# A two-layer mixer encoder: early gates' weights, residual stores, modulations and last down tiles rearranged

## The chip, the cores and the metric

The kernel runs on one core of one Trainium2 chip. The time is the device time of one execution in microseconds; three runs of the kernel before gave a median of 3291.7 us (3289.4 to 3296.47). Engines are called TensorE (PE in the rows; PEld is its weight load), VectorE (DVE), ScalarE (ACT), GpSimd (POOL) and SyncE (SP, which issues most DMAs).

## The reference

A trunk of two layers on x of 1024 tokens by 1024 features, all in float32. Each layer adds two gated sub-layers to x. Six vectors (shift, scale and gate of each) come from a conditioning vector c.

```python
D_MODEL = 1024; SEQ = 1024; DEPTH = 2; D_FF = 2816
for l in range(DEPTH):
    mod = (c_act @ w_mod[l] + b_mod[l])[:, None, :]
    sh1, sc1, g1, sh2, sc2, g2 = jnp.split(mod, 6, axis=-1)
    h = rms_norm(x, norm_g[l, 0]) * (1 + sc1) + sh1
    parts = jnp.split(h @ w_in[l], split_idx, axis=-1)
    # oa: windowed attention, ob: gated short convolution, oc: latent attention, od: dilated attention
    y = jnp.concatenate([oa, ob, oc, od], axis=-1) @ w_out[l]
    x = x + g1 * rms_norm(y, norm_g[l, 1])
    h = rms_norm(x, norm_g[l, 2]) * (1 + sc2) + sh2
    u = dwconv3(h @ w_up[l], ffn_conv[l])
    ug, uv = jnp.split(u, 2, axis=-1)
    y = (jax.nn.gelu(ug, approximate=True) * uv) @ w_down[l]
    x = x + g2 * rms_norm(y, norm_g[l, 3])
```

## The kernel before

Activations lie transposed: features on the 128 partitions in eight tiles, tokens along the free axis in two halves of 512 (`HALVES`). Each float32 product is three matmuls: both operands are split into a high and a low part (`split`: ScalarE copies the high part, L110, another engine subtracts it, L111; GpSimd where none is named). A layer runs in these stages (us of the profiled execution, layer 0 | layer 1):

- mixer: group A, the rotary tables (layer 0 alone), group D (from 177 | 1837), convolution B, latent attention C (its values from 614 | 2245). `group_d` projects three sets of values and takes a step of the iterator `fill` ahead of each. In layer 0 `fill` is `modulations`: the jobs j = 2, 4, 3 (a gate, a scale, a shift) of layer 0's own modulation. A job is `mod_pieces`, 16 loads of 256 KB (L357) each followed by a multiply-add on VectorE (L360, L362), and `mod_fold`. The loads go into slots of two tiles `room`, which later hold scores of group D.
- `project_out`: the mixer's output projection, first token half, second token half; ScalarE evicts each tile (L1165). Between the halves `residual` (L510 to L515: load of x, scale, add, store to `xd`) and `dense_input` (the norm and the shift, and for the second half the sums that the gates' fast product needs) of the first half run; behind it those of the second half, the *chain* (884 to 944 | 2514 to 2577).
- `dense_up`: 22 gates, each of a gate tile and a value tile of w_up. The product of a gate by two halves of tokens and of features is done with seven quarter products (`quarter`, 12 matmuls each) instead of eight, as in Strassen's scheme. `begin` does two of them, evicted by ScalarE (L1238, L1242). For the first 8 gates (`ahead`) `begin` is run early and its result kept in DRAM (`kept`), so that TensorE has work during the chain; two weights are loaded ahead of the chain (`early`). Then gates 0 and 1 are finished together and gates 2 to 7 one after the other with 60 matmuls, the *kept gates* (about 1012 to 1150 | 2622 to 2760); from gate 8 on `begin` and the rest are run in one, 84 matmuls, the *full gates* (to about 1416 | 3005). `sums` prepares sums of weights on VectorE, `taken` and `tail` read the product banks (L1280, L1281 on ScalarE, L1293 to L1299), `gated` convolves both tiles (`conv3`: L934 on ScalarE or L936 on VectorE, then twice L938), and multiplies the gelu (L1307) of one by the other (L1308, stored at L1309).
- Behind each full gate of layer 0 `advance(3)` issues three of the modulation pieces that `modulate` holds, six jobs: layer 0's j = 5 and layer 1's 1, 0, 2, 4, 3. What is left is issued during the down projection.
- `dense_down`: the 22 tiles of hidden features in chunks. `whole` multiplies a chunk into all eight output tiles; the first chunk is copied to y (L1410), others are added. In layer 0 the last six go by token half, in chunks of two (`some`, adds at L1417), so that layer 0's end and layer 1's start of the first half run beside the second half's products.

The order on each engine is made by a scheduler when the program is built; each engine then runs its own list in order. The DMAs that SP issues wait in SP's list for their slots or data.

Of the kernel before, what the change touches and what calls it, by code (L numbers as in the profile page):

```python
# [92 lines left out]
class Trunk:  # L93
# [369 lines left out]
    def dense_input(self, y, l, half, temp, adders):  # L463
# [20 lines left out]
        for i in range(4):  # L484
# [11 lines left out]
            self.split(self.hh[j][:, n2], self.hl[j][:, n2], b[:, n2])  # L496
# [5 lines left out]
    def residual(self, y, l, g, hs, xsrc, dst, temp, adders=None, rs=None):  # L502
# [3 lines left out]
        for k in range(KT):  # L506
# [8 lines left out]
            nc.sync.dma_start(dst[128 * k:128 * k + 128, hs], yk)  # L515
# [353 lines left out]
    def modulations(self):  # L869

        tiles = [self.sp.tile([128, 2048], F32, name="room", tag=t) for t in ("s10", "s11")]
        room = [t[:, at:at + 512] for t in tiles for at in range(0, 2048, 512)]
        for j in (2, 4, 3):
            pieces = self.mod_pieces(0, j, room)
            try:
                while True:
                    next(pieces)
            except StopIteration as done:
                part = done.value
            yield  # L880
            self.mod_fold(part, room[2])
# [215 lines left out]
    def mixer(self, l):  # L1097
        tc, nc = self.tc, self.nc
        with ExitStack() as e:
# [4 lines left out]
            with ExitStack() as e2:  # L1104
# [9 lines left out]
                self.group_d(l, self.modulations() if l == 0 else iter(()))  # L1114
# [91 lines left out]
    def dense_up(self, l, early):  # L1206
# [12 lines left out]
        ahead = 8  # L1219
        kept = self.kept  # L1220
        with tc.tile_pool(name=f"ux{l}", bufs=2, reuse_waits="tile") as ux, \
# [45 lines left out]
            class Pair:  # L1267
# [21 lines left out]
                def tail(p):  # L1289
# [8 lines left out]
                    nc.gpsimd.tensor_add(uv[:, c2], uv[:, c2], uv[:, c1])  # L1298
# [3 lines left out]
            def gated(t, us):  # L1302
                cv = [self.tmp(x) for x in "ab"]
                for o, u, m in zip(cv, us, (t, FT + t)):
                    base = _P["fconv"] + l * 132 + m
                    self.conv3(o, u, lambda i: self.par[:, base + 44 * i:base + 44 * i + 1], True)
# [33 lines left out]
            for t in range(2, FT):  # L1340
# [8 lines left out]
                if t >= ahead:  # L1349
                    self.advance(3)  # L1350

    def dense_down(self, l, y, end):
# [3 lines left out]
        with tc.tile_pool(name=f"dq{l}", bufs=4, reuse_waits="tile") as dq:  # L1356
# [25 lines left out]
            def load_half(ks, hs, names):  # L1382
# [4 lines left out]
                for k, wd, t in zip(ks, wds, next(room)):  # L1387
# [10 lines left out]
            def whole(ops, first):  # L1398
                for m in range(8):
                    if m:  # L1400
                        self.advance(1 if len(ops) < 4 else 2)
# [7 lines left out]
                    for d, p in [(y[m], po)] if po else [(y[m][:, h], q) for h, q in zip(HALVES, ps)]:  # L1409
                        self.mark = nc.vector.tensor_copy(d, p) if first else nc.vector.tensor_add(d, d, p)  # L1410
# [27 lines left out]
            else:  # L1438
                final, part = [range(at, at + 2) for at in range(k, FT, 2)], slice(0, 512)
                for ks in final:  # L1440
                    some(load_half(ks, HALVES[0], "ppp"), HALVES[0], part)
# [3 lines left out]
                rest = [load_half(ks, HALVES[1], names) for ks, names in zip(final, ("wwq", "qqq", "fff"))]  # L1445
                end(HALVES[0])()
                for ops in rest:
                    some(ops, HALVES[1], part)
                end(HALVES[1])()

    def run(self):
# [47 lines left out]
        for l in range(DEPTH):  # L1499
# [8 lines left out]
            with tc.tile_pool(name=f"fw{l}", bufs=3, reuse_waits="tile") as self.fw:  # L1508
                self.project_out(l, y, token_half(0, t))
                self.turn = cycle((0, 0, 0, 1, 1))  # L1510
                self.pieces = self.modulate([(0, 5), (1, 1), (1, 0), (1, 2), (1, 4), (1, 3)] if l == 0 else [])
                with tc.tile_pool(name=f"te{l}", bufs=1, reuse_waits="tile") as self.te:
                    early = [self.up_weight(l, t) for t in range(2)]
# [94 lines left out]
```

## Time and profile before

| | |
|---|---|
| median of three runs | 3291.7 us |
| lowest, highest | 3289.4, 3296.47 us |
| the profiled execution, its own time | 3296.84 us |
| its span | 3295.0 us |
| its granted TensorE clock, mean | 0.95 of full speed |
| TensorE busy | 2898.2 us (88%) |
| VectorE busy | 2293.4 us (70%) |
| ScalarE busy | 1219.3 us (37%) |
| GpSimd busy | 1208.9 us (37%) |

The profiled execution is one of the kernel as it stands, by the hardware profiler. A row of waits says which instruction stood still, on whose result, and for how long in all, how often, and the longest. A row of a stretch gives its bounds, its length, and each engine's busy time in it.

### The profile page before, as it was taken

To read this page: it belongs to the slowest core of one execution; us is meant where nothing else is said; L and a number is where in the kernel's file an instruction comes from. 1 tells how busy PE (TensorE), PEld (TensorE's weight loads), DVE (VectorE), ACT (ScalarE), POOL (GpSimd) and SP (SyncE) were. 2 spreads that over 40 slices of the span, in tenths; PEclk is the share of its full clock that TensorE was granted. 3 is DMA by queue.
4 is the path that set the end of the run, shared out by engine and by line. 5 is a ranking of instruction groups with operands and counts; after the bars stand their busy time and mean duration, and the time that the engine had idled before them with its cause. 6 is when DMAs were issued, how large, how long until landed. Compare 5 with 4: busy or idle time off the path is not lost. (4 is left out here: it accounts for less than half of the span.)

```text
span 3295.0 us, 35545 instructions
## 1 busy us (share of the span) xinstructions
PE 2898.2 (88%) x13178; PEld 2295.2 (70%) x13178; DVE 2293.4 (70%) x3120; ACT 1219.3 (37%) x1726; POOL 1208.9 (37%) x877
## 2 busy tenths in 40 slices
PE   7888889988858898989888998888897889998997
PEld 3677667776646777768756787677675667776886
DVE  6686666796648777786886735577966696666456
ACT  4222433554433333331233333435534333443121
POOL 1221223224445544552432212242244555555331
PEclk8998999999879999999999999999999899999999
DMA  5235111102423233355431121110123332223323
GB/s 199 80 104 169 55 33 47 39 20 77 147 90 115 94 111 112 107 200 163 160 125 41 52 83 52 42 41 26 52 93 125 115 122 77 77 77 139 129 90 102
DMA packets 124409, 311.62 MB, mean 95 GB/s; under 512 B 13595, under 2 KB 32283, under 8 KB 124236
## 3 DMA queue, kind: packets, MB, share of 16 engines
q1 hardware_dynamic: 121932, 300.97, 27.7%
q10 hardware_dynamic: 2304, 8.39, 0.6%
q8 instruction: 103, 1.69, 0.2%
q14 instruction: 70, 0.57, 0.1%
HBM read 248.58 MB, written 64.13 MB: 95 GB/s over the span
## 5 line engine op out<-in xcount | busy, mean ns | idle before, releaser
L111 POOL TENSOR_TENSOR wl<-raw,wh 128x1024 fp32r<-128x1024 f32 (+2 forms) x82 | 201.4, 2457 | 467.5 <-ACT wh L110 277.1
L530 PE MATMUL pj<-hh,wh 128*128 128x512 f32 x800 | 330.0, 413 | 15.0 <-DVE ql L579 8.4
L531 PE MATMUL pj<-hl,wh 128*128 128x512 f32 x800 | 323.1, 404 | 5.6 <-POOL hl L459 3.9
L534 PE MATMUL pj<-hh,wl 128*128 128x512 f32 x800 | 208.9, 401 | 0.0
L530 PEld LDWEIGHTS pj<-hh,wh 128*128 128x128 f32 x800 | 154.8, 193 | 56.7 <-issue 15.8
L531 PEld LDWEIGHTS pj<-hl,wh 128*128 128x128 f32 x800 | 154.7, 193 | 43.1 <-POOL hl L459 5.5
L534 PEld LDWEIGHTS pj<-hh,wl 128*128 128x128 f32 x800 | 153.0, 192 | 35.6 <-issue 0.9
L690 PE MATMUL po<-s,v 128*96 128x128 f32 (+3 forms) x672 | 130.7, 357 | 45.0 <-ACT s L687 45.0
L111 POOL TENSOR_TENSOR ul<-raw,uh 128x1024 fp32r<-128x1024 f32 x51 | 130.2, 2556 | 93.9 <-ACT uh L110 93.7
L690 PE MATMUL po<-hp,v 128*96 128x256 f32 x512 | 125.0, 399 | 38.3 <-ACT hp L687 38.1
L110 ACT ACTIVATE wh<-raw 128x1024 fp32r<-128x1024 f32 (+2 forms) x90 | 94.1, 1046 | 167.9 <-PE pj L531 76.5
L690 PEld LDWEIGHTS po<-s,v 128*96 128x96 f32 x672 | 98.7, 186 | 71.0 <-ACT s L687 55.7
L577 ACT ACTIVATE qh<-pj 64x512 fp32r<-64x512 f32 x128 | 107.1, 837 | 97.0 <-PE pj L534 51.5
L938 DVE SCALAR_TENSOR_TENSOR ta<-u,par,ta 128x1024 f32<-128x1024 f32 x88 | 135.8, 1543 | 3.4 <-ACT ta L934 3.2
L938 DVE SCALAR_TENSOR_TENSOR tb<-u,par,tb 128x1024 f32<-128x1024 f32 x88 | 136.7, 1553 | 0.3
L579 DVE TENSOR_TENSOR ql<-pj,qh 64x512 fp32r<-64x512 f32 x64 | 55.4, 866 | 116.5 <-ACT qh L577 115.8
L690 PEld LDWEIGHTS po<-hp,v 128*96 128x96 f32 x512 | 85.0, 171 | 72.9 <-ACT hp L687 46.5
L1410 DVE TENSOR_TENSOR y<-y,po 128x1024 f32<-128x1024 f32 x60 | 73.0, 1217 | 87.6 <-PE po L523 87.6
L561 DVE TENSOR_TENSOR ks<-pj,ks 64x512 fp32r<-64x512 f32 x56 | 51.1, 913 | 108.8 <-ACT ks L560 108.2
L111 POOL TENSOR_TENSOR pl<-raw,ph 128x1024 fp32r<-128x1024 f32 x26 | 67.2, 2591 | 147.5 <-ACT ph L110 104.4
L362 DVE SCALAR_TENSOR_TENSOR mc<-mr,cact,mc 128x512 f32<-128x512 f32 x98 | 107.1, 1092 | 17.6 <-DMA mr<-in_w_mod_dram 17.1
L677 PE MATMUL psc<-qh,ks 128*128 128x256 f32 (+2 forms) x272 | 86.1, 333 | 35.3 <-DVE s L805 15.1
(617 smaller groups left out, 8971.7 us busy)
## 6 DMA issues: line engine op xcount, KB each, us to landing
mr<-in_w_mod_dram SPq DMA_DIRECT2D x144, 256.0 KB, 3.0
raw<-in_w_up_dram SPq DMA_DIRECT2D x60, 512.0 KB, 3.6
raw<-in_w_in_dram SPq DMA_DIRECT2D x52, 512.0 KB, 3.3
raw<-in_w_down_dram SPq DMA_DIRECT2D x50, 512.0 KB, 3.9
actd<-ta SPq DMA_DIRECT2D x44, 512.0 KB, 2.6
uh<-in_w_up_dram SPq DMA_DIRECT2D x26, 512.0 KB, 4.2
room<-in_w_mod_dram SPq DMA_DIRECT2D x48, 256.0 KB, 3.8
xd<-y SPq DMA_DIRECT2D x48, 256.0 KB, 2.6
```

The source lines that it names most:

```text
L110: self.nc.scalar.activation(hi, src, AF.Copy)
L111: (eng or self.nc.gpsimd).tensor_sub(lo, src, hi.bitcast(F32))
L362: nc.vector.scalar_tensor_tensor(acc, w, s, acc, op0=ALU.mult, op1=ALU.add)
L530: nc.tensor.matmul(ps, wh[:, ks], self.hh[k][:, hs], start=k == 0, stop=False, skip_group_check=True)
L531: nc.tensor.matmul(ps, wh[:, ks], self.hl[k][:, hs], start=False, stop=False, skip_group_check=True)
L534: nc.tensor.matmul(ps, wl[:, ks], self.hh[k][:, hs], start=False, stop=k == KT - 1, skip_group_check=True)
L577: nc.scalar.activation(self.perm(qh[h][o:o + 64], r)[:, n * half:n * half + n, :], src, AF.Copy)
L579: nc.vector.tensor_sub(lo, src, own.bitcast(F32))
L677: nc.tensor.matmul(ps, ks[:, c], qh[:, q0:q1], start=first, stop=False, skip_group_check=True)
L690: nc.tensor.matmul(o[0:96, co], v(tt, h), s[:, cs], start=co.start // 512 not in seen, stop=False, skip_group_check=True)
L938: nc.vector.scalar_tensor_tensor(o, t[:, i:i + n], cw(i), o, op0=ALU.mult, op1=ALU.add)
L1410: self.mark = nc.vector.tensor_copy(d, p) if first else nc.vector.tensor_add(d, d, p)
```

## The change

Eight edits:

1. In the second half's `dense_input`, the four splits of `b[:, n2]`, all on GpSimd, go to VectorE for even i.
2. `residual` issues its stores to `xd` from ScalarE's queue; stores to the output stay on SP.
3. `modulations` runs in both layers' mixers, each for its own layer. Layer 0's gates issue no pieces any more; three jobs (layer 0's j = 5, layer 1's 1 and 0) are left, and they run in layer 0's down projection, behind its first chunk.
4. `ahead` is 6 instead of 8, and five weights, not two, are loaded ahead of the chain.
5. The add of `tail` at L1298 goes from GpSimd to VectorE.
6. The convolutions' first multiply stays on ScalarE for the gate tiles of gates 0 to 7; the other 72 of 88 go to VectorE.
7. The last six down tiles of layer 0 are taken in chunks of 4 and 2 for the first token half and of 6 for the second (before: 2, 2, 2 each).
8. The first down chunk's copies go from VectorE to ScalarE (L1409 in the new numbering).

```diff
@@ dense_input
-            self.split(self.hh[j][:, n2], self.hl[j][:, n2], b[:, n2])
+            self.split(self.hh[j][:, n2], self.hl[j][:, n2], b[:, n2], nc.gpsimd if i % 2 else nc.vector)
@@ residual
-            nc.sync.dma_start(dst[128 * k:128 * k + 128, hs], yk)
+            (nc.sync if dst is self.a["out"] else nc.scalar).dma_start(dst[128 * k:128 * k + 128, hs], yk)
@@ modulations
-    def modulations(self):
+    def modulations(self, l):
-            pieces = self.mod_pieces(0, j, room)
+            pieces = self.mod_pieces(l, j, room)
@@ mixer
-                self.group_d(l, self.modulations() if l == 0 else iter(()))
+                self.group_d(l, self.modulations(l))
@@ dense_up
-        ahead = 8
+        ahead = 6
-                    nc.gpsimd.tensor_add(uv[:, c2], uv[:, c2], uv[:, c1])
+                    nc.vector.tensor_add(uv[:, c2], uv[:, c2], uv[:, c1])
-                    self.conv3(o, u, lambda i: self.par[:, base + 44 * i:base + 44 * i + 1], True)
+                    self.conv3(o, u, lambda i: self.par[:, base + 44 * i:base + 44 * i + 1], m == t < ahead + 2)
-                if t >= ahead:
-                    self.advance(3)
@@ dense_down
-                for k, wd, t in zip(ks, wds, next(room)):
+                for k, wd, t in zip(ks, wds, [t for pair in room for t in pair]):
-                    if m:
+                    if m and not first:
-                        self.mark = nc.vector.tensor_copy(d, p) if first else nc.vector.tensor_add(d, d, p)
+                        if first:
+                            self.mark = nc.scalar.activation(d, p, AF.Copy)
+                        else:
+                            self.mark = nc.vector.tensor_add(d, d, p)
-                final, part = [range(at, at + 2) for at in range(k, FT, 2)], slice(0, 512)
-                for ks in final:
-                    some(load_half(ks, HALVES[0], "ppp"), HALVES[0], part)
+                part = slice(0, 512)
+                for ks, names in ((range(k, k + 4), "pppppp"), (range(k + 4, FT), "ppf")):
+                    some(load_half(ks, HALVES[0], names), HALVES[0], part)
-                rest = [load_half(ks, HALVES[1], names) for ks, names in zip(final, ("wwq", "qqq", "fff"))]
+                ops = load_half(range(k, FT), HALVES[1], "wwqqqqfff")
-                for ops in rest:
-                    some(ops, HALVES[1], part)
+                some(ops, HALVES[1], part)
@@ run
-                self.pieces = self.modulate([(0, 5), (1, 1), (1, 0), (1, 2), (1, 4), (1, 3)] if l == 0 else [])
+                self.pieces = self.modulate([(0, 5), (1, 1), (1, 0)] if l == 0 else [])
-                    early = [self.up_weight(l, t) for t in range(2)]
+                    early = [self.up_weight(l, t) for t in range(5)]
```

Three places show how the change moves instructions. The first is SP's list in layer 1's group D, around the last weight of the values (`in_w_dv`); `vd` and `row` are values on their way through DRAM. Before:

```order
L116 DMA raw<-in_w_in_dram 128x1024 x2
L116 DMA raw<-in_w_dv_dram 128x1024
L663 DMA bias<-brep_90 128x256
L645 DMA vd_87<-row 128x260 x2
L663 DMA bias<-brep_91 128x384
L645 DMA vd_87<-row 128x260 x2
L654 DMA v<-vd_87 128x260 x2
L645 DMA vd_87<-row 128x260
L654 DMA v<-vd_87 128x260 x2
L645 DMA vd_87<-row 128x260 x3
L116 DMA raw<-in_w_dv_dram 128x1024
```

And now:

```order
L654 DMA v<-vd_87 128x260
L645 DMA vd_87<-row 128x260
L654 DMA v<-vd_87 128x260 x3
L357 DMA room<-in_w_mod_dram 128x512
L645 DMA vd_87<-row 128x260
L357 DMA room<-in_w_mod_dram 128x512 x2
L645 DMA vd_87<-row 128x260
L357 DMA room<-in_w_mod_dram 128x512 x3
L645 DMA vd_87<-row 128x260
L357 DMA room<-in_w_mod_dram 128x512 x3
L654 DMA v<-vd_87 128x260 x4
L357 DMA room<-in_w_mod_dram 128x512 x3
L116 DMA raw<-in_w_dv_dram 128x1024
```

All 48 loads of pieces stand ahead of that weight now, mixed with the values' stores and loads.

The second is ScalarE's list at the end of layer 0's chain; the last rows of the chain are the splits of `x` (t1) and `sq` (t3), and L1238 evicts the third and fourth begun gate. Before:

```order
L474 ACTIVATE y<-y,mod 128x512
L110 ACTIVATE hp<-y 128x512
L110 ACTIVATE hp<-x 128x512
L110 ACTIVATE t_6560<-t 128x512
L110 ACTIVATE y<-x 128x512
L110 ACTIVATE y<-sq 128x512
L1238 ACTIVATE u<-pj 128x512 x2
```

And now:

```order
L474 ACTIVATE y<-y,mod 128x512
L110 ACTIVATE hp<-x 128x512
L110 ACTIVATE hp<-y 128x512
L110 ACTIVATE t_6578<-t 128x512
L110 ACTIVATE y<-x 128x512
L110 ACTIVATE y<-sq 128x512
L1238 ACTIVATE u<-pj 128x512 x2
```

Both evictions stand behind the chain as they did.

The third is the start of layer 0's down projection. Before, VectorE's list, where L938 convolves the last gate and L362 are pieces:

```order
L1299 TENSOR_TENSOR u<-u,po 128x512
L938 SCALAR_TENSOR_TENSOR ta<-u,par,ta 128x1024
L938 SCALAR_TENSOR_TENSOR tb<-u,par,tb 128x1024
L938 SCALAR_TENSOR_TENSOR ta<-u,par,ta 128x1024
L938 SCALAR_TENSOR_TENSOR tb<-u,par,tb 128x1024
L1410 COPY y<-po 128x1024
L1308 TENSOR_TENSOR ta<-ta,tb 128x1024
L362 SCALAR_TENSOR_TENSOR mc<-mr,cact,mc 128x512
L1410 COPY y<-po 128x1024
L362 SCALAR_TENSOR_TENSOR mc<-mr,cact,mc 128x512
L1410 COPY y<-psc 128x512 x2
```

And now ScalarE's, where `ph<-raw` splits a weight and `ph<-pl` an act tile:

```order
L110 ACTIVATE ph<-raw 128x1024
L1409 ACTIVATE y<-po 128x1024
L110 ACTIVATE ph<-pl 128x1024
L110 ACTIVATE ph<-raw 128x1024
L1409 ACTIVATE y<-po 128x1024
L1307 ACTIVATE ta<-ta 128x1024
L1409 ACTIVATE y<-psc 128x512 x2
L110 ACTIVATE ph<-pl 128x1024
L110 ACTIVATE ph<-raw 128x1024
L1409 ACTIVATE y<-po 128x1024 x2
L1409 ACTIVATE y<-psc 128x512
L110 ACTIVATE ph<-pl 128x1024
```

The copies have left VectorE's list, where they stood behind the convolution, for ScalarE's, where they stand between splits and the last gate's gelu.

## Rows read from the trace of the kernel before

**Rows 1.** The page's busy time of each engine, share of the span, instructions.

```profile
PE 2898.2 (88%) x13178; PEld 2295.2 (70%) x13178; DVE 2293.4 (70%) x3120; ACT 1219.3 (37%) x1726; POOL 1208.9 (37%) x877
```

**Rows 2.** Stretches: bounds, length; busy us PE, PEld, DVE, ACT, POOL; clock, DMA, GB/s.

```profile
177.10:614.00 436.90, 381.37 (x1989) 317.80 (x1988) 303.98 (x461) 147.45 (x208) 108.66 (x70) 0.94 0.25 80
210.00:300.00 90.00, 68.07 (x381) 59.08 (x380) 82.25 (x154) 23.71 (x42) 22.18 (x17) 0.88 0.65 208
1012.00:1150.00 138.00, 120.31 (x496) 96.07 (x496) 117.51 (x103) 54.94 (x62) 72.10 (x67) 0.94 0.32 111
1150.00:1416.00 266.00, 247.48 (x1044) 196.53 (x1042) 203.81 (x222) 104.38 (x125) 130.87 (x108) 0.99 0.34 112
1600.00:1652.00 52.00, 42.54 (x172) 33.23 (x172) 45.70 (x56) 14.72 (x20) 21.87 (x13) 0.93 0.41 138
1837.10:2245.00 407.90, 370.10 (x1983) 308.98 (x1983) 239.64 (x334) 145.02 (x204) 107.60 (x70) 0.97 0.17 53
1870.00:1960.00 90.00, 85.71 (x492) 73.28 (x491) 33.10 (x59) 34.87 (x51) 25.90 (x19) 1.00 0.26 81
2760.00:3005.00 245.00, 237.82 (x1020) 190.18 (x1018) 152.78 (x156) 101.77 (x122) 129.60 (x106) 1.00 0.23 80
```

**Rows 3.** TensorE's waits, us in all, times, longest; 1150 to 1416, 2760 to 3005.

```profile
PE po L1200 <- ACT u L1281: 11.0, 6, 2.9
...
PE po L1200 <- ACT u L1281: 6.0, 7, 1.2
```

**Rows 4.** VectorE's waits from 2760 to 3005, layer 1's full gates.

```profile
DVE u L1299 <- POOL u L1298: 51.1, 12, 7.0
DVE raw L1262 <- POOL vl L111: 33.7, 10, 4.3
```

**Rows 5.** Durations in ns, min/median/max; the last is the page's, mean ns.

```profile
L936 DVE TENSOR_SCALAR u<-u,par x2: 711/711/711, 584.2 to 2214.9; 128x1024 f32<-128x1024 f32 x2
L934 ACT ACTIVATE ta<-u,par x44: 1132/1148/1157, 1010.0 to 3015.0; 128x1024 f32<-128x1024 f32 x44
L1298 POOL TENSOR_TENSOR u<-u x44: 1265/1296/2271, 994.0 to 3012.9; 128x512 f32<-128x512 f32 x44
L362 DVE SCALAR_TENSOR_TENSOR mc<-mr,cact,mc x98: 733/750/2958, 1153.6 to 3077.2; 128x512 f32<-128x512 f32 x98
L362 DVE SCALAR_TENSOR_TENSOR mc<-mr,cact,mc 128x512 f32<-128x512 f32 x98 | 107.1, 1092 | 17.6 <-DMA mr<-in_w_mod_dram 17.1
```

**Rows 6.** VectorE in order of time, layer 1's group D: start, us, idle before.

```profile
1941.04 1.10 DVE L561 TENSOR_TENSOR ks<-pj,ks 64x512 fp32r<-64x512 f32 x1 [25.08 <-ACT ks L560]
```

**Rows 7.** TensorE's wait from 880 to 945, and ScalarE in order of time.

```profile
PE pj L1200 <- ACT u L1238: 33.1, 1, 33.1
...
943.78 0.61 ACT L110 ACTIVATE y<-sq 128x512 fp32r<-128x512 f32 x1
944.30 0.58 ACT L1238 ACTIVATE u<-pj 128x512 f32<-128x512 f32 x1
```

**Rows 8.** TensorE's waits from 2506 to 2575, layer 1's chain.

```profile
PE pj L1200 <- ACT u L1242: 6.8, 1, 6.8
PE pj L1200 <- ACT u L1238: 6.2, 1, 6.2
```

**Rows 9.** TensorE's waits, 1412 to 1470, 3000 to 3060; ScalarE by time.

```profile
PE po L521 <- DVE y L1410: 9.5, 3, 4.7
...
PE po L521 <- DVE y L1410: 7.3, 3, 6.8
...
1441.29 1.06 ACT L110 ACTIVATE ph<-pl 128x1024 fp32r<-128x1024 f32 x1 [10.38 <-DMA pl<-actd]
```

**Rows 10.** TensorE's waits from 1600 to 1652; L1417's durations in ns.

```profile
PE pd L521 <- DVE y L1417: 9.5, 4, 5.3
...
L1417 DVE TENSOR_TENSOR y<-y,pd x72: 372/674/691, 1612.3 to 3275.7; 128x512 f32<-128x512 f32 x56, 128x256 f32<-128x256 f32 x16
```

**Rows 11.** SP's issues of the residual stores, ns, min/median/max.

```profile
L515 SPq DMA_DIRECT2D xd<-y x48: 319/320/432, 829.3 to 2535.0; - x48
```

## The prediction

> **What bounds the kernel now.** I read the busy shares first, then a table of stretches, then the waits inside the stretches that the diff touches. TensorE is busy 88% of the span [rows 1]; the reader should look for the other 397 us, since an edit elsewhere pays only where TensorE stands still. The table [rows 2] shows where it does: the attention of group D in layer 0, the kept gates, the full gates of layer 0, the end of layer 0's down projection. Then I ask which wait ends last. In the full gates it is ScalarE's copy L1281 [rows 3]; at the down projection's start VectorE's copies [rows 9]; in the second half's chain one wait of 33.1 us for an eviction [rows 7]. Last I ask whether VectorE has room, since six of the edits lean on it [rows 4, 5].
>
> **1. Three modulations leave layer 0's gates.** Full gates need 84 matmuls. Layer 0 runs 1044 in 266 us, 0.2548 us each; layer 1, with the same gates and no pieces, 1020 in 245 us, 0.2402 each [rows 2]. The difference times 1044 is 15 us. Of it 11 us is TensorE's idle time (18.5 against 7.2), the rest slower matmuls at a slightly lower granted clock (0.99 against 1.00). I take **-15** (-11 to -19; the high end adds pieces that stand among the first down tiles).
>
> **2. They return in layer 1's mixer.** 48 pieces at 0.75 us alone and 1.09 in the mean [rows 5] are 36 to 52 us of VectorE, and 48 loads of 256 KB on SP's queue. Layer 0 shows the price, because it already runs such a set there: from 210 to 300 TensorE is idle 21.9 us, in layer 1's like stretch 4.3 [rows 2], 17.6 apart. From the first value matmul to the latent values layer 0 takes 436.9 us, layer 1 407.9: 29 is the upper end, some of it the rotary table. For less speaks that VectorE idles 25.08 us in one piece in layer 1 there, waiting on keys [rows 6]; if the pieces fit, 4 remain. Against that, SP's order puts the last values' second weight behind all 48 loads, and each load waits for a slot that VectorE must free. I take **+16** (+4 to +29).
>
> **3. The full gates.** ScalarE loses two multiplies of 1.15 us a gate (they are on VectorE from gate 8 on, one of two before), and TensorE's remaining 7.2 us in layer 1's stretch are nearly all waits for ScalarE's L1281, 6.0 [rows 2, 3]. Half of it should go: -3 per layer, **-6**. VectorE pays. A gate of layer 1 has 12.6 us of VectorE busy (152.78 over 12.14 gates) and 7.0 of waits for GpSimd (51.1 and 33.7 over 12.14) [rows 2, 4], 19.6 of a 20.2 us pace. The 4.2 us wait for L1298 goes with the hop to GpSimd; added are two multiplies of 0.711 and one add at 0.68, the duration of the like add L1417 [rows 5, 10], 2.1 together. That gives 12.6 + 2.8 + 2.1 = 17.5, or 18.5 if the three cost 1.46 times as much, L362's mean over its median, 1.092 over 0.750 [rows 5]. TensorE needs 19.6 (237.82 over 12.14), so VectorE stays behind it, by little. Bounds: -14 (all idle time of both layers) to +6.
>
> L362, which has two streams from SBUF, takes from 0.733 to 2.958 us for one shape [rows 5]. The Trainium skill ("SBUF — State Buffer", section "SBUF: two separate sides") says that a VectorE operation with two SBUF inputs, or in a two-port mode, and a GpSimd operation exclude each other for the whole instruction. That speaks against moving work to VectorE: with GpSimd busy 47% of this stretch (129.60 less twelve L1298, of 245 us) and 2.4 us operations, each of the three would wait some 0.56 us more on average, an estimate, and the gate would be 19.2 us of VectorE instead of 18.5. The trace's spread fits the rule; it makes the third rival below likelier and leaves this term's sign.
>
> **4. Kept gates, six instead of eight.** TensorE is idle 17.7 us of 138 there in layer 0 [rows 2], about 8.3 gates of 60 matmuls, 2.1 us each; a full gate loses 7.2 over 12.14, 0.6. Two gates converted save 3 per layer. The remaining ones get 0.711 and 0.68 more on VectorE, which is busy 117.51 of 138 already, less the hop. I take -2 per layer, **-4** (-8 to +2).
>
> **5. The second half's chain.** In layer 0 the eviction of the third begun gate starts at 944.30, right behind the last split of the chain, and TensorE has waited 33.1 us for it [rows 7]. The loads of five weights come earlier now, but in the new order on ScalarE the same eviction still stands behind all of the chain, so TensorE has the same two begun gates for cover and the wait stays: **0** (-4 to +4, for two splits more on VectorE and two less on GpSimd). In layer 1 the waits are 6.2 and 6.8 [rows 8]; there the two evictions L1238 stood after 9 operations of the chain and now stand after some 16, which at 0.6 to 0.7 us each is 5 us later: **+5** (0 to +8).
>
> **6. The first down tiles' copies on ScalarE.** TensorE waits 9.5 us in layer 0 and 7.3 in layer 1 for L1410, copies that stand behind the last gate's convolution on VectorE [rows 9]. On ScalarE two copies come ahead of that gate's gelu and the others before TensorE asks for their banks again. I take -8 and -6, **-14** (-17 to -4). The low end is a new wait: ScalarE's split of an act tile once waited 10.38 us for its DMA [rows 9], and now copies are queued behind such splits; from the third act tile on, two chunks' rows of output hang on it.
>
> **7. Layer 0's last down tiles.** 48 adds become 24, at 0.674 us 16 us less of VectorE, which is busy 45.70 of 52 us from 1600 to 1652; TensorE waits 9.5 us there for these adds [rows 2, 10]. With 12 or 18 matmuls per output tile instead of 6, an add has twice or three times as long. I take **-8** (-14 to +2, where six weights needed at once come late).
>
> **8. Residual stores on ScalarE's queue.** 48 issues of 0.32 us, 15 us in all [rows 11], go from SP to ScalarE. In each layer's first half eight of them stand ahead of evictions of the output projection, eight of the second half in the chain. What waits behind a store waits for the residual's add too, mostly work that needs that add anyway. **+3** (0 to +10).
>
> **The sum**: -15 + 16 - 6 - 4 + 0 + 5 - 14 - 8 + 3 = -23. On the profiled execution, 3296.84 us (span 3295.0), that is 3274; this execution is 5.1 above the median of 3291.7, so against the median it is **3269**. The terms' half-widths (4, 12, 10, 5, 4, 4, 6, 8, 5), added as squares, give 21: 3248 to 3290 for this case alone.
>
> **Rivals.** *Covered hole.* The early weights do let TensorE work through the 33.1 us wait: 3 more would leave of it, so 30 less, **3239**. For it: five weights are ready. Against: it waits for an eviction, not for a weight, and the eviction's place is unchanged.
>
> *Moved, not removed.* Layer 1's mixer pays all 29 us as layer 0 does (+13 on the sum), and the copies wait behind act tiles' DMAs on ScalarE (-4 instead of -14, +10): -23 + 23 = 0, **3292**. For it: the same program in layer 0 pays it; SP's order keeps a weight behind all loads. Against: the 25 us gap.
>
> *VectorE sets the gates' pace*, which ends slower. The place is the gate loop of both layers. The price: if one moved operation's wait for GpSimd is nearer L362's longest (2.958) than its mean, the gate's VectorE time passes TensorE's 19.6 us; the point is 1.1 us a gate above my 18.5. VectorE with pieces (203.81 over 12.43 gates, 16.4 us busy) went with layer 0's pace of 0.2548; at that pace in both layers term 1 is lost (+15), terms 3 and 4 too (+10), and layer 1 loses 1020 x 0.0146 = 15: -23 + 40 = +17, **3309**. For it: layer 0 itself, and VectorE busy or waiting all but 0.6 us of layer 1's gate. Against: the 4.2 us wait that goes is more than what is added.
>
> **How the numbers follow.** Forecast 0.58, covered hole 0.07, moved 0.18, VectorE's pace 0.17. About 0.2%, 6.6 us, can be told from no change: faster is under 3285, slower over 3298. Of the forecast 0.55 lies under 3285 and 0.03 above; of "moved" 0.03 faster, 0.12 the same, 0.03 slower; of VectorE's pace 0.03 the same, 0.14 slower. Faster 0.65, same 0.18, slower 0.17. The range of 8 in 10 leaves out most of the covered hole and the upper part of VectorE's pace: 3244 to 3303.
>
> **What the profile after would show.** Step 1: the full gates of both layers within 0.24 us per matmul. Step 2: idle TensorE, pieces and waits of value matmuls from 1850 to 1980, 10 to 20 us more than now. Step 3: no wait for L1298, VectorE near 15 us busy a gate, TensorE's waits for L1281 halved. Step 5: a wait of some 33 us for L1238. Step 6: waits for the first copies under 3 us a layer. Step 7: waits for L1417's adds under 3 us at layer 0's end. I am wrong if the gates' pace rises to 0.25 in layer 1, if the 33 us wait is gone, or if ScalarE waits on DMAs with copies queued behind.

## The result and the profile after

The changed kernel takes 3239.66 us (median of four runs, 3239.33 to 3242.23) against 3294.09 before on the same chip: 0.9836 of the time, 95% interval 0.9818 to 0.9853. That is 54 us faster, where 23 were forecast; 3239.66 lies below the stated range of 3244 to 3303. The rival *covered hole* had given 3239 for another reason, and that reason did not come about: the 33 us wait in layer 0's chain is still there. That its number fits is luck.

The profiled execution after has a span of 3240.4 us. Its page gives the busy times that answer to [rows 1]:

```profile
PE 2884.5 (89%) x13178; PEld 2291.8 (71%) x13178; DVE 2385.1 (74%) x3196; ACT 1159.5 (36%) x1674; POOL 1157.2 (36%) x821
```

VectorE took over work and is busy 92 us more in a shorter span; TensorE's share rose by a point. The stretches that answer to [rows 2] (bounds, length; busy us and instructions of TensorE, its weight load, VectorE, ScalarE, GpSimd; granted clock, DMA share, GB/s), in the order kept gates of layer 0, full gates of layer 0, values of layer 1, full gates of layer 1:

```profile
1005.00:1080.00 75.00, 64.52 (x269) 50.77 (x267) 74.36 (x68) 25.24 (x28) 34.32 (x33) 0.98 0.35 120
1100.00:1360.00 260.00, 258.52 (x1121) 210.26 (x1120) 221.85 (x214) 86.67 (x111) 132.02 (x112) 1.00 0.23 81
1779.00:1955.00 176.00, 152.34 (x915) 133.47 (x914) 133.65 (x225) 50.19 (x86) 32.15 (x29) 0.94 0.41 129
2690.00:2950.00 260.00, 259.89 (x1130) 212.01 (x1129) 225.79 (x215) 86.84 (x110) 134.12 (x107) 1.00 0.25 87
```

The full gates are now TensorE's alone: busy 258.5 and 259.9 of 260 us, 0.230 us per matmul in layer 1 where it was 0.240, at a granted clock of 1.00. The kept gates are VectorE's: 74.36 of 75. In layer 1's values TensorE stands still for 24 us.

Where the 54.5 us of the span lie, by the first start of marked instructions in the two traces (TensorE's first matmul of the line, where nothing else is said):

| mark | before | after | difference | from the mark above |
|---|---|---|---|---|
| second half's residual, layer 0 (VectorE, L513) | 888.6 | 888.5 | -0.1 | -0.1 |
| first finished gates, layer 0 (L1333) | 973.4 | 962.9 | -10.5 | -10.4 |
| down projection, layer 0 (L521) | 1414.3 | 1381.6 | -32.7 | -22.2 |
| its second chunk | 1450.0 | 1406.3 | -43.7 | -11.0 |
| first half-tile adds (VectorE, L1417, now L1418) | 1612.3 | 1569.5 | -42.8 | +0.9 |
| values, layer 1 (L637) | 1837.1 | 1779.1 | -58.0 | -15.2 |
| last of the values, layer 1 | 1986.7 | 1953.5 | -33.2 | +24.8 |
| second half's residual, layer 1 | 2517.9 | 2484.3 | -33.6 | -0.4 |
| first finished gates, layer 1 | 2584.4 | 2544.7 | -39.7 | -6.1 |
| down projection, layer 1 | 3011.7 | 2964.3 | -47.4 | -7.7 |
| its second chunk | 3044.7 | 2990.2 | -54.5 | -7.1 |
| last add | 3275.7 | 3221.2 | -54.5 | 0 |

Two begun gates (48 matmuls, some 11 us) moved in each layer from ahead of the mark L1333 to behind it. Without that the chains cost +0.5 and +4.8, and the gate loops gained 33 and 18.6 us.

TensorE's waits over the whole span after, of the lines on which the change bears (us in all, times, longest; other lines are left out):

```profile
PE pj L1200 <- ACT u L1238: 39.5, 3, 29.6
PE po L158 <- ACT sq L164: 23.9, 11, 8.2
PE psc L1200 <- DVE u L1280: 23.3, 8, 4.1
PE pj L530 <- DVE ks L561: 14.7, 5, 5.1
PE pd L521 <- DVE y L1418: 4.9, 2, 2.9
PE po L521 <- ACT y L1409: 3.9, 4, 2.1
PE po L1200 <- ACT u L1281: 2.3, 2, 1.4
```

The wait of [rows 7] is 29.6 us now. Those of [rows 3] for L1281 are nearly gone, those of [rows 9] and [rows 10] for copies and adds are down to 3.9 and 4.9. Longer are L561, the subtraction behind layer 1's keys (3.1 before), and L164, the squares of the chain (13.3 before).

### The profile page after: what moved, and what is told of

It is laid out like the page before. It is cut to its first block, busy times and chain, and to the rows that moved or that the text cites. A ratio compares the mean times of both kernels' runs of the same rounds, so it can differ in the third digit from the quotient of the medians.

```text
span 3240.4 us, 35414 instructions
## 1 busy us (share of the span) xinstructions
PE 2884.5 (89%) x13178; PEld 2291.8 (71%) x13178; DVE 2385.1 (74%) x3196; ACT 1159.5 (36%) x1674; POOL 1157.2 (36%) x821
## 5 line engine op out<-in xcount | busy, mean ns | idle before, releaser
L690 PE MATMUL po<-s,v 128*96 128x128 f32 (+3 forms) x672 | 133.4, 360 | 43.8 <-ACT s L687 43.7
L111 POOL TENSOR_TENSOR ul<-raw,uh 128x1024 fp32r<-128x1024 f32 x45 | 120.6, 2680 | 70.2 <-ACT uh L110 70.1
L938 DVE SCALAR_TENSOR_TENSOR ta<-u,par,ta 128x1024 f32<-128x1024 f32 x88 | 138.9, 1578 | 1.4 <-ACT ta L934 1.4
L938 DVE SCALAR_TENSOR_TENSOR tb<-u,par,tb 128x1024 f32<-128x1024 f32 x88 | 128.2, 1457 | 0.0
L677 PE MATMUL psc<-qh,ks 128*128 128x256 f32 (+2 forms) x272 | 88.3, 339 | 38.9 <-DVE s L805 15.2
L560 ACT ACTIVATE ks<-pj 64x512 fp32r<-64x512 f32 x56 | 49.0, 876 | 163.8 <-PE pj L534 96.5
L561 DVE TENSOR_TENSOR ks<-pj,ks 64x512 fp32r<-64x512 f32 x56 | 51.0, 911 | 73.6 <-ACT ks L560 72.8
```

The lines of the kernel that those rows point to most:

```text
L111: (eng or self.nc.gpsimd).tensor_sub(lo, src, hi.bitcast(F32))
L677: nc.tensor.matmul(ps, ks[:, c], qh[:, q0:q1], start=first, stop=False, skip_group_check=True)
L690: nc.tensor.matmul(o[0:96, co], v(tt, h), s[:, cs], start=co.start // 512 not in seen, stop=False, skip_group_check=True)
L938: nc.vector.scalar_tensor_tensor(o, t[:, i:i + n], cw(i), o, op0=ALU.mult, op1=ALU.add)
```

## The experiments

All ratios are to the kernel before on the same chip, with 95% intervals; the changed kernel's is 0.9836. 0.001 is 3.3 us. The intervals reach 0.0013 to 0.0025 to either side, so two ratios that differ by under some 0.0025 are not told apart. "Undone" is one edit taken out of the changed kernel.

**The add of `tail` back on GpSimd.**

```diff
-                    nc.vector.tensor_add(uv[:, c2], uv[:, c2], uv[:, c1])
+                    nc.gpsimd.tensor_add(uv[:, c2], uv[:, c2], uv[:, c1])
```

> The changed kernel with one edit undone: tail's add L1298 goes back from VectorE to GpSimd. Theory A (the gate loops were bound by VectorE's list, which stood still 4.2 us a gate for this hop; the change won most there): 20 to 35 us slower than the changed kernel's 3239.7, so 3260 to 3275, with VectorE's waits for L1298 back. Rival B (the gain is ScalarE's, whose copy L1281 held TensorE): at most 8 us slower, 3240 to 3248.

0.9980 (0.9967 to 0.9994), 3294.9 us: nearly all of the gain is gone, more than either theory said. Layer 0's gate loop takes 440.1 us to the copies (969.1 to 1409.2) instead of 421.7. In 2720 to 2990, layer 1's full gates, VectorE and TensorE wait:

```profile
DVE u L1299 <- POOL u L1298: 32.3, 13, 5.0
DVE u L1297 <- PE po L1204: 29.1, 12, 4.5
...
PE po L1200 <- ACT u L1281: 9.1, 6, 2.0
```

VectorE stands 2.5 us a gate for the hop (its wait for the add on GpSimd), in the middle of its list, and TensorE's wait for L1281 is back although ScalarE has no more work than in the changed kernel. So VectorE's list was behind that wait too: theory A (the rows that show how stand under step 3 below).

**The first multiplies back on ScalarE.**

```diff
-  self.conv3(o, u, lambda i: ..., m == t < ahead + 2)
+  self.conv3(o, u, lambda i: ..., True)
```

> The changed kernel with one edit undone: all 88 first multiplies of the gates' convolutions back on ScalarE. Theory A: VectorE gets 1.4 to 2 us a gate back and no wait ends later, so 3235 to 3243. Rival B: ScalarE's list holds TensorE at L1281 again, 20 to 30 us slower, 3260 to 3270.

0.9815 (0.9800 to 0.9830), 3238.7 us: not told apart from the changed kernel, a little faster if anything. Beside what it costs VectorE, ScalarE's relief was worth nothing. VectorE's busy time in layer 1's full gates falls from 225.79 to 194.03 of 260 us, and TensorE is busy 259.76 us where it was 259.89.

**Both back.**

> The changed kernel with both edits undone: the add back on GpSimd and the multiplies back on ScalarE. Theory A: about as the run with the add alone undone, a little faster, 3258 to 3272. Rival B: as the run with the multiplies alone undone, 3260 to 3272, with L1281 as TensorE's main wait. If neither edit alone is worth much but both are, the two cover for each other, and this run alone is slow.

0.9938 (0.9918 to 0.9959), 3279.5 us. With the hop on GpSimd, taking the multiplies off VectorE recovers some 14 us; without the hop it recovers nothing. The two edits share VectorE's list. By this the multiplies' move without the hop's would have cost time; no run put it into the kernel before by itself.

**The add alone, put into the kernel before.**

> The kernel before with one edit alone: tail's add L1298 on VectorE instead of GpSimd. Theory A (VectorE's list, its waits for the hop included, set the pace of the gates): 20 to 40 us faster than the kernel before, 0.988 to 0.994 of its time, the gain in both gate loops. Rival (the hop counts only once ScalarE's multiplies and the pieces are gone): under 10 us faster, 0.997 to 1.

0.9925 (0.9906 to 0.9944), 3272.1 us: 25 us from one word. By the marks, 8.8 us in layer 0's gate loop, where the pieces still stand in VectorE's list, and 15.3 in layer 1's. A stretch of layer 1's full gates, and VectorE's longest wait in it:

```profile
2735.00:2985.00 250.00, 250.00 (x1088) 204.26 (x1087) 188.69 (x178) 108.15 (x131) 123.57 (x100) 1.00 0.25 83
...
DVE raw L1262 <- POOL vl L111: 38.5, 11, 4.4
```

TensorE does not wait here any more, for L1281 or anything else. VectorE's other wait for GpSimd, L1262, is still there and costs nothing.

**The modulations back in layer 0's gates.**

```diff
-                self.group_d(l, self.modulations(l))
+                self.group_d(l, self.modulations(l) if l == 0 else iter(()))
@@ dense_up
+                if t >= ahead:
+                    self.advance(3)
@@ run
-                self.pieces = self.modulate([(0, 5), (1, 1), (1, 0)] if l == 0 else [])
+                self.pieces = self.modulate([(0, 5), (1, 1), (1, 0), (1, 2), (1, 4), (1, 3)] if l == 0 else [])
```

> The changed kernel with one edit undone: layer 1's jobs 2, 4, 3 are issued from layer 0's gates again, three pieces behind each full gate, and the rest in the down projection; layer 1's mixer has none. Layer 1's values then take 25 us less, as in the kernel before. Theory A: VectorE with pieces passes TensorE's 19.6 us a gate again, layer 0's gates lose 10 to 20 us, so 3225 to 3236. Rival: VectorE is fuller than before the change, the gates lose all 25 us or more, 3238 to 3255.

0.9857 (0.9840 to 0.9873), 3252.6 us, 7 us slower by the ratio, which is within what is not told apart, and 13 by the medians. The trace shows both sides: layer 1's values take 149.4 us instead of 174.4, layer 0's gate loop 446.0 instead of 418.7. The gates lose all of the 25 us, the rival's case. VectorE is nearly full there, in 1100 to 1380:

```profile
1100.00:1380.00 280.00, 262.94 (x1110) 210.94 (x1109) 266.82 (x273) 81.09 (x105) 134.47 (x104) 0.98 0.33 111
```

**Layer 0's last tiles in chunks of two again.**

> The changed kernel with one edit undone: layer 0's last six down tiles in chunks of two again. If the bigger chunks and the halved number of adds are worth what layer 0's end shows between the two traces, 8 to 15 us slower than 3239.7: 3248 to 3255, with TensorE waiting for the adds again. If that gain came from other edits (the pieces gone from the down projection's end), under 4 us: 3238 to 3243.

0.9912 (0.9888 to 0.9936), 3270.5 us, 25 us slower by the ratio, more than expected. Parts that the edit does not touch came 7 us later in this profile by layer 0's chain; from the first half-tile adds to the first projection of layer 1 it takes 93.8 us, the changed kernel 77.9, the kernel before 86.4. TensorE's wait for the adds there (2.0 us in the changed kernel):

```profile
PE pd L521 <- DVE y L1418: 16.6, 4, 6.4
```

So some 16 us of the 25 lie where the edit works. The kernel before, with the same chunks of two, took only 8.5 us longer there than the changed kernel, so how much of the 16 the edit is worth by itself stays open.

**Two more banks for begun gates** (an addition to the changed kernel).

```diff
-  x = self.pj.tile([128, 512], F32, name="pj", tag="pj")
+  x = self.psc.tile(..., tag="psc") if other else self.pj.tile(..., tag="pj")    # other: t > 3
```

> The changed kernel with one addition: the fifth and sixth begun gate use the PSUM banks of pool psc instead of pj. If the wait of 29.6 us in layer 0's chain is for a bank whose eviction stands behind the chain on ScalarE, and not for weights, TensorE has two more begun gates to run and the wait falls by 10 to 20 us, layer 1's chain by up to 5: 3218 to 3232. If the wait is for something else, 3237 to 3242.

0.9815 (0.9793 to 0.9836), 3237.9 us: no gain that can be told. Yet the 29.6 us wait is broken up, and the first finished gates start at 945.4 instead of 962.9. The waits from 880 to 1110 show what is late next:

```profile
PE psc L1334 <- ACT uh L110: 14.2, 2, 13.1
PE psc L1200 <- DVE u L1281: 12.2, 4, 4.1
PE psc L1200 <- ACT u L1239: 5.4, 1, 5.4
```

The gate that TensorE reaches early waits 13.1 us for a weight's split, and then VectorE's pace rules (79.36 busy of the 80 us from 1000). At the down projection's start 0.8 of the 17.5 us are left. The cause of the wait is shown, a bank whose eviction stands late; covering it is not worth 30 us but nothing that can be told.

**The three jobs spread over mixer, gates and down projection.**

```diff
-        for j in (2, 4, 3):
+        for j in (2, 4, 3) if l == 0 else (2,):
-                self.pieces = self.modulate([(0, 5), (1, 1), (1, 0)] if l == 0 else [])
+                self.pieces = self.modulate([(1, 4), (0, 5), (1, 1), (1, 0), (1, 3)] if l == 0 else [])
@@ dense_up: self.advance(1) behind a full gate; dense_down: advance(3) instead of 2 in chunks of four; conv3(..., True)
```

> The changed kernel with the convolutions' first multiplies all on ScalarE and layer 1's three moved jobs spread: j = 2 in layer 1's mixer, j = 4 one piece behind each full gate of layer 0, j = 3 in layer 0's down projection. If the mixer's loss of 25 us comes from VectorE's list being full there (key subtractions behind pieces), two thirds of it come back and the gates, with the multiplies away from VectorE, hold 16 pieces free: 3220 to 3230. If VectorE is as full in the other places, the pieces cost as much there: 3236 to 3246.

0.9934 (0.9910 to 0.9958), 3276.7 us: a miss, 32 us slower. The down projection from its second chunk to the half tiles takes 192.6 us instead of 163.2; TensorE waits 18.7 us for adds, and VectorE for the pieces' loads, from 1400 to 1610:

```profile
PE po L521 <- DVE y L1413: 18.7, 6, 6.7
...
DVE mc L362 <- DMA mr<-in_w_mod_dram: 28.6, 31, 2.5
```

And the mixer with a third of the pieces still pays 15 of its 25 us. The pieces' cost was not proportional to their number here, and a list that waits for loads cost in the down projection too.

**Eight kept gates again.**

> The changed kernel with one edit undone: eight gates are begun early again, not six (the multiplies stay as in the change, on ScalarE for the gate tiles of gates 0 to 7). If a kept gate costs what the two traces say (5 to 6 us a layer in all between six and eight), 8 to 13 us slower than the changed kernel's 3239.7: 3248 to 3253. If it is worth what the prediction's step 4 gave, 4 us: 3242 to 3246.

0.9931 (0.9915 to 0.9947), 3274.6 us: 31 us slower by the ratio, some three times what the traces had made me expect and eight times step 4. Layer 0's gate loop takes 418.2 us with 48 matmuls fewer in it, as long as the changed kernel's 418.7, and layer 1's 418.0 instead of 419.6. What the two gates put ahead of the loop is lost whole: from the second half's residual to the first finished gates it takes 13.8 us longer in layer 0 and 17.1 in layer 1. In 1000 to 1110 VectorE is busy 105.86 of 110 us.

**The copies back on VectorE.**

> The changed kernel with one edit undone: the first down chunk's copies on VectorE again. The time from the first matmul of the down projection to the second chunk's fell by 11.0 us in layer 0 and 7.1 in layer 1; if the copies' place is the cause, 14 to 20 us slower: 3253 to 3260, with TensorE's waits for them back. If the gain comes from the pieces that no longer stand among them (layer 0) and from the freer VectorE (both), under 8: 3240 to 3248.

0.9849 (0.9833 to 0.9865), 3249.2 us, 4 to 10 us slower by ratio or median; the ratio alone does not tell it apart. In the profile layer 0's first chunk takes 31.0 us instead of 24.7 (35.7 before), layer 1's 31.6 instead of 25.9 (33.0 before). In layer 0 there is one wait for a copy:

```profile
PE po L521 <- DVE y L1409: 6.4, 1, 6.4
```

By these marks the copies' place is worth about 6 us in each layer. The other 5 of layer 0's 11 are by subtraction those of other edits; which ones, no run shows.

**Two early weights.**

> The changed kernel with one edit undone: two weights, not five, are loaded ahead of the chain. If the wait in the chain is for a bank and the begun gates behind it do not wait for weights, 3236 to 3244. If the earlier weights carry part of the gain in the begun gates, 5 to 15 us slower: 3245 to 3255.

0.9832 (0.9817 to 0.9846), 3242.5 us: the same. The three extra weights ahead of the chain are worth nothing that can be told.

**The residual stores back on SP's queue.**

```diff
-            (nc.sync if dst is self.a["out"] else nc.scalar).dma_start(dst[128 * k:128 * k + 128, hs], yk)
+            nc.sync.dma_start(dst[128 * k:128 * k + 128, hs], yk)
```

> The changed kernel with one edit undone: the residual stores on SP's queue again. The prediction gave the edit 3 us of cost, so undone 3236 to 3238; if the time of the stages around the residuals, which hardly moved between the traces, tells all, 3238 to 3242; if the loads that stand behind the stores on SP matter, 5 us slower or more: over 3244.

0.9800 (0.9781 to 0.9819), 3230.1 us: 10 to 12 us faster than the changed kernel, so the edit costs three to four times what step 8 said. ScalarE in order of time in layer 1's chain, changed kernel (start, us, idle before; ACTq is its issue of DMAs):

```profile
2487.93 0.63 ACT L164 ACTIVATE sq<-y 128x512 f32<-128x512 f32 x1 [1.59 <-POOL y L514]
2491.40 4.99 ACTq L515 DMA_DIRECT2D xd<-y  x4
2496.73 0.63 ACT L164 ACTIVATE acc<-y 128x512 f32<-128x512 f32 x1 [8.16 <-DVE y L513]
2497.26 1.13 ACT L164 ACTIVATE sq<-y 128x512 f32<-128x512 f32 x2
```

Four stores, each behind its own add, stand ahead of the squares; ScalarE does nothing for 8.16 us, and TensorE's sums wait 8.2. With the stores on SP the same squares are spread over these 8 us, and TensorE's longest wait for one of them in that chain is 2.3 us.

**Four kept gates; four with the stores on SP; that and all multiplies on ScalarE; three with the stores on SP.**

> The changed kernel with four gates begun early and kept instead of six (and four early weights; the multiplies stay as they are). If a kept gate is paced by VectorE (74.36 busy of 75 us there) and the begun gates are no cover for the wait in the chain, two more converted gates a layer bring 5 to 8 us a layer: 3222 to 3232. If six is near the point where TensorE runs out of begun gates during the chain, or a kept gate costs what step 4 gave it, 3235 to 3245.

> The changed kernel with four gates kept and the residual stores on SP's queue again. If the stores on ScalarE's queue cost some 10 us in the chains and layer ends, and that has nothing to do with the gates, the two add up: 10 us under the run with four gates kept alone, 3212 to 3222. If the run with the stores alone was faster by a luckier order in layer 1's chain, no faster than four gates kept alone.

> The changed kernel with four gates kept, the stores on SP and all first multiplies on ScalarE. If VectorE's list paces the kept gates alone and TensorE the full gates, the multiplies' place is worth under 4 us beside the run without that edit.

> The changed kernel with three gates kept and three early weights, the stores on SP. TensorE runs two begun gates and the first quarter of a third before the chain's evictions hold it, so a fourth gate is no cover: 3 to 4 us a layer faster than the run with four kept and the stores on SP. If the fourth gate's begin is cover in layer 1's chain, where evictions stand among the chain's rows, the same or slower.

0.9825 (0.9805 to 0.9845), 0.9799 (0.9774 to 0.9824), 0.9790 (0.9767 to 0.9813) and 0.9824 (0.9804 to 0.9845); 3237.0, 3228.4, 3225.0 and 3236.1 us. Four kept gates bring layer 0's down projection 5.7 us forward, as expected of one layer, but layer 1 takes 479.8 us from the second half's residual to the down projection where six kept gates take 480.0: not told apart from six. Three are slower than four by 8 us, all in layer 1: layer 0's down projection starts at 1375.7 in both. From layer 1's second residual to its down projection three take 480.5 us, four 474.1, so that the fourth begun gate is no cover does not hold there; about as much of the loss lies ahead of that stretch and is not explained. The stores on SP give 9 us more beside four kept gates, where the order is another, so their cost is not one lucky order. The multiplies' place is worth nothing here either.

The third is faster than both kernels: 3225.0 us, 0.979 of the kernel before. Its interval ends just below the changed kernel's.

## Why the prediction was wrong

**Step 3 failed in the price that it put on the hop. Together with step 4, and with step 1 in layer 0, it is nearly the whole miss**: -6 and -4 forecast, with step 1's -15 some -25 for the gate loops; measured -52. In layer 1, which step 1 does not touch, -5 was forecast and -18.6 measured. The numbers in step 3 were right: 12.6 us busy and 7.0 us of waiting make 19.6 of a gate's 20.2 us. The step that failed is what I drew from them: I priced the edit by TensorE's idle time left in one stretch, 7.2 us, of which I took half, and put that idle time down to ScalarE's work. The kernel before, layer 1, in order of time over three engines:

```profile
2793.51 0.69 DVE L1299 TENSOR_TENSOR u<-u,po 128x512 f32<-128x512 f32 x1 [3.52 <-POOL u L1298]
...
2802.86 0.68 DVE L1258 TENSOR_TENSOR wl<-wl,wh 128x512 f32<-128x512 f32 x1
2803.63 1.06 ACT L110 ACTIVATE uh<-wl 128x1024 fp32r<-128x1024 f32 x1 [2.53 <-DVE wl L1258]
...
2805.12 0.58 ACT L1281 ACTIVATE u<-po 128x512 f32<-128x512 f32 x1
2805.75 0.50 PE L1200 MATMUL po<-hp,uh 128*128 128x512 f32 x1 [0.87 <-ACT u L1281]
```

VectorE works without a gap from L1299, which stood 3.52 us for the hop, to L1258. ScalarE waits for L1258, its L1281 comes two rows later, and TensorE waits for L1281. So TensorE's wait for ScalarE, on which the step rested, was the tail of VectorE's list, and moving the multiplies away from ScalarE changed nothing. The time of one full gate in each run (from the start of gate 7's gelu to gate 21's, by 14, in us) shows what the list was worth:

| | layer 0 | layer 1 |
|---|---|---|
| kernel before | 21.6 | 20.5 |
| hop alone moved | 21.2 | 19.7 |
| changed kernel | 19.7 | 19.6 |
| its hop undone | 20.9 | 20.9 |
| its multiplies undone | 19.5 | 19.5 |
| hop and multiplies undone | 20.3 | 20.5 |
| modulations back in layer 0's gates | 21.4 | 19.7 |

In layer 1 the hop is nearly all of the full gates' gain. In layer 0 the hop alone (20.9) and the pieces alone (21.2, 21.4) each still hold the gates back, so both had to go. The sum of VectorE's busy time and its waits for GpSimd, 97% of the pace, pointed at the list but proves nothing by itself: TensorE was busy 97% of the same stretch, and with the hop undone in the changed kernel the sum is 17.5 of 20.4 us a gate while the loop is slow all the same. The runs with and without the hop decide it.

Three things made the size wrong further. First, the stretch began behind the first full gates; by the gelus of gates 7 and 21 (1125.10 and 1427.17, 2736.23 and 3023.2) the pace before was 21.6 and 20.5 us, not 21.4 and 20.2. Second, idle time was not all that there was to win: over layer 0's whole gate loop TensorE is busy 401.6 us for 1669 matmuls before and 401.2 us for 1717 after, at a granted clock of 0.97 and 0.99. Third, step 4 took a kept gate for TensorE's (2.1 us idle of 60 matmuls) and asked what TensorE loses. In the changed kernel VectorE is busy 74.36 of 75 us in these gates, so the 24 matmuls that a kept gate leaves to be done ahead of the loop do not shorten the loop, and undoing the edit costs 31 us. The undoings add up to far more than the gain (the hop 47, kept gates 31, tiles 25 by the ratios); the edits are not independent, as the table shows of the hop and the pieces.

The third rival, that VectorE sets the pace, was wrong of the direction: VectorE's list held the gates back already in the kernel before, and the change took that away in the full gates. Its price rested on contention with GpSimd, and that was real. VectorE, then GpSimd, in order of time, kept gates of the changed kernel:

```profile
1044.47 3.42 DVE L938 SCALAR_TENSOR_TENSOR ta<-u,par,ta 128x1024 f32<-128x1024 f32 x1
...
1054.27 2.85 DVE L936 TENSOR_SCALAR tb<-u,par 128x1024 f32<-128x1024 f32 x1
...
1060.63 1.27 DVE L938 SCALAR_TENSOR_TENSOR tb<-u,par,tb 128x1024 f32<-128x1024 f32 x1
...
1043.14 3.67 POOL L111 TENSOR_TENSOR ul<-ul,uh 128x1024 fp32r<-128x1024 f32 x1 [8.00 <-issue]
...
1053.94 2.63 POOL L111 TENSOR_TENSOR ul<-wh,uh 128x1024 fp32r<-128x1024 f32 x1
```

The moved multiply takes 2.85 us where [rows 5] had 0.711, a convolution step 3.42 instead of 1.27, both 2.1 us more. The two long ones begin while a GpSimd split runs and end 1.1 and 0.6 us after it, about what they take alone. The Trainium skill ("SBUF — State Buffer", section "SBUF: two separate sides") has a VectorE operation with two SBUF inputs, or in a two-port mode, and a GpSimd operation that reads SBUF exclude each other for the whole instruction. These rows agree with it. Contention did not decide the change: in the full gates TensorE is busy all the time with the multiplies on either engine. VectorE's busy time a full gate of layer 1 came to 16.8 us (225.79 over 1130 matmuls by 84) where "near 15" was said, still under the 19.3 that TensorE works on it.

**Step 1** had the right sign and at least its size: putting the pieces back costs layer 0's gates more than the 25 us that they cost in layer 1's mixer. With the hop gone, the pieces cost 1.7 us a gate of layer 0 (21.4 against 19.7), some 24 us for fourteen gates. It can't be told from steps 3 and 4 more exactly, since they share VectorE.

**Step 2**: +24.8 against +16, inside its bounds, near the upper one. Of it 17.2 us are TensorE's idle time and 7.6 slower matmuls, at a granted clock of 0.94 where it was 1.00. The 25.08 us gap of [rows 6] did not hide the pieces. The keys' subtractions stand between them in VectorE's list, and TensorE waits for those, not for the weight that I named. TensorE's longest wait from 1779 to 1955 (0.7 us in the like stretch before), then VectorE, GpSimd and TensorE in layer 1's values:

```profile
PE pj L530 <- DVE ks L561: 12.2, 3, 5.1
...
1838.12 2.60 DVE L360 TENSOR_SCALAR room<-room,cact 128x512 f32<-128x512 f32 x1
1840.64 2.82 DVE L362 SCALAR_TENSOR_TENSOR room<-room,cact 128x512 f32<-128x512 f32 x1
1843.49 0.69 DVE L561 TENSOR_TENSOR ks<-pj,ks 64x512 fp32r<-64x512 f32 x1
...
1837.78 2.66 POOL L111 TENSOR_TENSOR s<-raw,s 128x1024 fp32r<-128x1024 f32 x1 [5.71 <-ACT s L110]
1840.40 2.52 POOL L111 TENSOR_TENSOR wl<-raw,wh 128x1024 fp32r<-128x1024 f32 x1
...
1844.33 0.77 PE L530 MATMUL pj<-hh,wh 128*128 128x512 f32 x1 [5.06 <-DVE ks L561]
```

Two pieces that last about as long as the two GpSimd splits beside them stand ahead of L561, and TensorE waits 5.06 us.

**Step 5** was right in layer 0: the 33 us wait stayed (29.6), and the chain cost +0.5 against 0. In layer 1 it was right by luck, +4.8 against +5. The evictions were to cost it, but TensorE's waits for them fell from 13.0 to 10.6 us there; those for the squares rose from 4.6 to 9.6, which is step 8's place. The rival *covered hole* fell twice: the wait is not for weights (two early weights are as good as five), and covering it is worth nothing that can be told.

**Step 6**: -11.0 and -7.1 against -8 and -6; by the undoing's marks the copies' place alone is worth 6.3 and 5.7. The new wait on act tiles came only as 3.9 us in all.

**Step 7** came out at -15.2 to the values of layer 1 against -8, just outside the bound of -14. Of that, 8.5 us lie ahead of layer 1's first projection, as forecast, and 6.7 behind it; the undoing shows 16 in the first part. Why the rest came is not shown.

**Step 8** was mis-sized the other way: 9 to 12 us against +3, near or past its upper bound of 10. The step's "What waits behind a store waits for the residual's add too, mostly work that needs that add anyway" was the wrong premise: the store of one tile stands ahead of the squares of others.

*Moved, not removed* fell; the mixer paid most of what it said (24.8 of 29), the copies did not, and the rest gained. The splits of edit 1 were not tried alone.

## What to carry to other kernels

Before pricing an edit, follow the busiest engine's wait back through the other engines' lists: here TensorE waited for a copy of ScalarE, which stood behind a split that waited for VectorE, which had stood for an add on GpSimd. An edit is worth what it takes out of such a chain, until the next limit comes. The hop had cost VectorE 4.2 us of waiting a gate; moving it alone brought layer 1's gates 0.8 us each, because TensorE was then busy all the time. The idle time left on the busiest engine in one stretch is no bound for it, if the stretch is cut short or the edit also changes what precedes the loop. Adding up an engine's busy time and its waits points at a list; moving the one instruction by itself decides. Before covering a long wait, ask what the next stage waits for: here 17.5 us of cover were given back before the next stage began, to an engine that was full. And look twice at stores on the queue of an engine whose next rows others wait for: here they cost 9 to 12 us.

## What the runs showed of the hardware

A VectorE multiply of 128x1024 from one SBUF tensor took 0.711 us while GpSimd was idle, and 2.85 when it began behind the start of a GpSimd split of 2.63 us; a convolution step took 3.42 instead of 1.27 beside a split of 3.67 us. The profile shows the longer time as busy time: VectorE's 74.36 of 75 us hold such operations, so an engine that looks full can in part be one that is kept from its work. In layer 0's gate loop TensorE's idle time fell from 39.3 to 17.5 us, and the granted clock of that stretch was 0.97 before and 0.99 after. Forty-eight issues of stores took 0.32 us each on SP's queue and 0.33 on ScalarE's, but on ScalarE's they stood in its order, and it computed nothing for 8.16 us around four of them.
